# Seven block products per pair: running sums in three PSUM banks, in place of seven buffers

## The chip, the core and the metric

One core of a Trainium2 chip runs the program. The metric is the device time of one execution in microseconds; the kernel before takes 883.73 us (median of three runs, 881.79 to 884.05). TensorE is written PE, VectorE DVE, ScalarE ACT, GpSimd POOL and SyncE SP.

## What is computed

One inference step of a one-layer hybrid recurrent decoder, on 544 tokens (512 of a prompt and 8 x 4 of samples) of width 1024, in float32:

```python
z = x @ p["w_in"]                       # 1024 -> 6144, split among branches and gates gl
out_a = (h * gelu(ya)) @ proj_a         # RG-LRU branch, after a convolution and a scan
out_b = (sb * cu) @ proj_b              # short convolution branch
out_c = (zc * sigmoid(zc @ glu_w + glu_b)) @ proj_c   # S5 state space branch
g = sigmoid(gl)                         # three gates of width 1024
m = g[0] * out_a + g[1] * out_b + g[2] * out_c
x = layer_norm(ALPHA * x + m @ w_out)
f = square(relu(x @ mlp_up)) @ mlp_down # 1024 -> 4096 -> 1024
x = layer_norm(ALPHA * x + f)
```

## The kernel before

Activations lie with channels on the partitions and the 544 tokens along the free axis. To keep float32 accuracy each operand is split into a high half (an ACT cast to fp32r) and a low half (a DVE subtract, value minus high half), and each product is three matmuls: high by high, high by low, low by high. Weights come as tiles of 128 x 1024 (512 KB): SP loads one into one of three raw buffers, ACT casts the high half (`split`, line 809; line 115 for the tiles of other stages), DVE subtracts the low half (line 810; 116), both into one of five weight buffers.

In two stages a group of 256 output channels is computed with a block scheme of seven products in place of eight. These are the gate projections of merge a (three of four quarters) and of merge c (four), and the up projection of the MLP (six of its eight groups of 512 channels, two pairs each): 19 pairs. The weights are cut into quarters A11 to A22, the activations into two halves of the channels and two of the tokens (N1 and N2, 272 tokens each). A pair takes four weight tiles: the first holds A11 and A12 as loaded, the second and third hold sums S1, S2 and S3, S4 that POOL forms from two raw tiles into the buffer "sr" (`p_s` in `add_pair`), the fourth A22. The matching sums of activations (`Tt`) are formed once per stage.

`pair7` is one pair. `prod` gives one product: 4 x 3 matmuls of 128 x 128 by 272 columns (line 844) into a PSUM bank. The order is P1, P2 (first weight tile), P6, P5 (second), P7, P3 (third), P4 (fourth). Each takes a new PSUM buffer by `big()`; there are four such buffers of two banks, which also serve all other matmuls of the stage. ACT copies P1 to p1 in SBUF; DVE adds (line 234, operands "big" and "uu") form u2 = P6 + p1, u4 = P5 + u2, u3 = P7 + u2 and the four result halves in `t` (tile "rl"): t[0] N1 = P2 + p1, t[1] N2 = P7 + u4, t[0] N2 = P3 + u4, t[1] N1 = P4 + u3. After the pair ACT applies tanh (merges) or relu (MLP) to both halves of t.

Weight preparation is a queue, `wq`: `take` gives the next tile, `done` releases one and has `pump` emit the next entry of `prep`, so that five tiles are prepared ahead. So in program order, behind the last product that reads a tile, stands the split of the tile five places on: in the MLP, where each pair is preceded by two tiles of the down projection (96 matmuls, line 147), the release of the pair's second tile (after P5) emits the split of the next pair's first tile. The framework lays out each engine's order from this program by priority and by readiness in its own model, and sets all waits; so an instruction can run ahead of one that is written before it, but only in an order that is fixed when the kernel is built. A wait is on a tile's or bank's earlier readers and writers.

In the merges a pair is followed or preceded by the projection `prj`, whose two PSUM buffers are held until DVE has multiplied them with the gate. In the last quarter of merge a the projection comes first.

Of the kernel before, what the change touches and what calls it, by code (L numbers as in the profile page):

```python
# [11 lines left out]
F32 = mybir.dt.float32  # L12
F32R = mybir.dt.float32r
I32 = mybir.dt.int32
AF = mybir.ActivationFunctionType
ALU = mybir.AluOpType
MUL, ADD, SUB = ALU.mult, ALU.add, ALU.subtract
# [6 lines left out]
H2 = T // 2  # L24
# [10 lines left out]
W2 = 1  # L35
# [30 lines left out]
def kernel(ctx: ExitStack, tc: tile.TileContext, I, O):  # L66
    nc = tc.nc
    V, S, G, PE = nc.vector, nc.scalar, nc.gpsimd, nc.tensor
# [19 lines left out]
    def big():  # L88
        return psb.tile([128, 2, 512], F32, tag="big", name="big")

    def flat(ps):
        return ps[:, :, 0:H2]

    def two(ap):
        return ap.rearrange("p (h n) -> p h n", h=2)
# [85 lines left out]
    for q in range(4):  # L181
# [10 lines left out]
        for e in range(2):  # L192
            k = 2 * q + e
# [39 lines left out]
    def tt(e, o, a, b, op):  # L233
        e.tensor_tensor(o, a, b, op=op)  # L234
# [541 lines left out]
        r.append(t_put(v))  # L776
        return r

    wq = {"prep": [], "n": 0, "live": 0, "t": [], "cap": 4 + W2, "pool": {}, "free": []}

    def pump():
        while wq["live"] < wq["cap"] and wq["n"] < len(wq["prep"]):
            wq["t"].append(wq["prep"][wq["n"]]())
            wq["n"] += 1
            wq["live"] += 1
        if wq["n"] == len(wq["prep"]):
            while wq["live"] < wq["cap"] and wst["sub"] < wst["lim"]:
                w_split(wst["sub"], wq["free"].pop(0))
                wst["sub"] += 1
                wq["live"] += 1  # L790
# [10 lines left out]
    def raw(i, j):  # L801
        w_raw(j)
        return wst["r"][i]

    def split(src, n=1024):
        pool = wq["free"].pop(0)
        h, l = wtile(pool)
        wq["pool"][id(h)] = pool
        S.copy(h[:, 0:n], src)  # L809
        V.tensor_tensor(l[:, 0:n], src, h[:, 0:n].bitcast(F32), op=SUB)  # L810
        return h, l
# [9 lines left out]
    def add_pair(i):  # L821
        sd = {}

        def p_s():
            a, b = raw(i, i), raw(i + 1, i)
            sr = srp.tile([128, 2048], F32, tag="sr", name="sr")
            A11, A12, A21, A22 = a[:, 0:512], a[:, 512:], b[:, 0:512], b[:, 512:]
            S1, S2, S3, S4 = (sr[:, 512 * q:512 * q + 512] for q in range(4))
            tt(G, S1, A21, A22, ADD)
            tt(G, S2, S1, A11, SUB)  # L830
            tt(G, S3, A11, A21, SUB)
            tt(G, S4, A12, S2, SUB)
            sd["s"] = sr
            return split(sr[:, 0:1024])

        wq["prep"] += [lambda: split(raw(i, i)), p_s, lambda: split(sd["s"][:, 1024:]),
                       lambda: split(raw(i + 1, i)[:, 512:], 512)]

    def prod(out, W, o, x):
        h, l = W  # L840
        for k in range(4):
            sl = slice(o + 128 * k, o + 128 * k + 128)
            for oi, (w, y) in enumerate(((h, x[0]), (h, x[1]), (l, x[0]))):
                PE.matmul(out, w[:, sl], y[:, k], start=k == 0 and oi == 0, stop=k == 3 and oi == 2)  # L844

    def pair7(X, Tt):
        t = [ttile(T, "rl") for _ in range(2)]
        uu = upp.tile([128, 4, H2], F32, tag="uu", name="uu")
        p1, u2, u3, u4 = (uu[:, i] for i in range(4))

        def Tx(i):
            return [Tt[i][:, 0], Tt[i][:, 1]]

        def mk():
            return big()[:, 0, 0:H2]

        P1, P2 = mk(), mk()
        Wa = take()
        prod(P1, Wa, 0, [x[:, :, N1] for x in X[0]])
        S.copy(p1, P1)  # L860
        prod(P2, Wa, 512, [x[:, :, N1] for x in X[1]])
        done(Wa)
        tt(V, t[0][:, N1], P2, p1, ADD)
        Ws = take()
        P6 = mk()
        prod(P6, Ws, 512, Tx(1))
        tt(V, u2, P6, p1, ADD)
        P5 = mk()
        prod(P5, Ws, 0, Tx(0))
        done(Ws)  # L870
        tt(V, u4, P5, u2, ADD)
        Wt = take()
        P7 = mk()
        prod(P7, Wt, 0, Tx(2))
        tt(V, u3, P7, u2, ADD)
        tt(V, t[1][:, N2], P7, u4, ADD)
        P3 = mk()
        prod(P3, Wt, 512, [x[:, :, N2] for x in X[1]])
        done(Wt)
        tt(V, t[0][:, N2], P3, u4, ADD)  # L880
        P4 = mk()
        Wz = take()
        prod(P4, Wz, 0, Tx(3))
        done(Wz)
        tt(V, t[1][:, N1], P4, u3, ADD)
        return t

    m = [stile(name="m") for _ in range(2)]
# [25 lines left out]
    def merge7(kh, kl, k4f, pl, out=None):  # L914
        nonlocal ti

        def prj():
            W = take()
            r = []
            for e in range(2):  # L920
                r.append(big())
                k4(outs_flat(r[e]), W, e, kh, kl)
            done(W)
            return r

        for q in range(4):
            if q in k4f:
                ps = prj()
                t = pair7(X0, Tt0)
            elif q in pl:  # L930
                ps, t, g = [], [ttile(T, "t") for _ in range(2)], []
                for e in range(2):
                    g.append(big())
                    W = take()
                    for k in range(KT):
                        sl = slice(k * 128, k * 128 + 128)
                        mm3(outs_flat(g[e]), k == 0, k == KT - 1, W[0][:, sl], W[1][:, sl], *X(k))
                    done(W)
                    S.copy(two(t[e]), flat(g[e]))
                ps = prj()  # L940
            else:
                t = pair7(X0, Tt0)
                ps = prj()
            for e in range(2):
                mt = 2 * q + e
                th, mm = t[e], M_(mt)
                S.activation(th, th, AF.Tanh, scale=0.5)
                V.scalar_tensor_tensor(two(th), two(th), 1.0, flat(ps[e]), op0=ADD, op1=MUL)
                if out is None:
                    tt(G, mm, mm, th, ADD)  # L950
                else:
                    tt(V, th, mm, th, ADD)
                    hd, ld = (x[mt // 4][:, mt % 4] for x in out)
                    S.mul(hd, th, 0.5)
                    V.scalar_tensor_tensor(ld, th, 0.5, hd.bitcast(F32), op0=MUL, op1=SUB)
                run_side(ti)
                ti += 1
# [52 lines left out]
    W = None  # L1010
# [173 lines left out]
    def up_pair(g, q):  # L1184
        if g not in fs:
            fs[g] = ([stile(F32R, name="fh")], [stile(F32R, name="fl")])
        fh, fl = fs[g][0][0], fs[g][1][0]
        t = pair7(X1, Tt1)
        for e in range(2):
            f, v = 2 * q + e, t[e]  # L1190
            S.activation(v, v, AF.Relu)
            S.activation(v, v, AF.Square)
            S.copy(fh[:, f], v)
            tt(V, fl[:, f], v, fh[:, f].bitcast(F32), SUB)
# [252 lines left out]
```

## Time and profile before

| | |
|---|---|
| median of three runs | 883.73 us (881.79, 883.73, 884.05) |
| profiled execution: its time, its span | 883.13 us, 881.4 us |
| PE busy | 841.1 us (95%), 6516 matmuls |
| DVE busy | 635.6 us (72%) |
| ACT busy | 370.7 us (42%) |
| POOL busy | 310.7 us (35%) |
| mean granted TensorE clock | 0.986 of full speed |
| chain that ended last | PE 73%, DVE 15%, POOL 4% of the span |

The span goes from the first to the last instruction. Matmuls are pipelined, and a busy PE need not run at its peak. The chain follows the work back from the last instruction, at each step to what released it. All times in rows are us from the start of the span.

### The profile page before, as it was taken

Reading aid. Unit: us, or ns where it says so; the run is one execution under the profiler, and the core shown is the slowest. Engines: PE = TensorE matmul, PEld = TensorE weight load, DVE = VectorE, ACT = ScalarE, POOL = GpSimd, SP = SyncE. Lnnn points to the kernel's source line nnn. Section 1 sums busy time; section 2 is a strip of 40 time slices with the busy share of each in tenths; the row PEclk is TensorE's granted clock in tenths of the full one; section 3 lists DMA queues with packets and bytes.
Section 4 is the critical chain, followed back from the end, with each engine's and each line's share of the span. In section 5 each row is a group of like instructions: output and inputs, shape, how many; then the busy total and the mean of one; then the engine's idle time right before and its main releaser. Section 6 shows DMA issues by size and latency. Waiting matters only on the chain.

```text
span 881.4 us, 16024 instructions
## 1 busy us (share of the span) xinstructions
PE 841.1 (95%) x6516; PEld 830.7 (94%) x6516; DVE 635.6 (72%) x1032; ACT 370.7 (42%) x626; POOL 310.7 (35%) x293
## 2 busy tenths in 40 slices
PE   7998598989999999979999999999999999999996
PEld 7997497979999999979998999999999999999996
DVE  6976998986756766689857889666666655656656
ACT  4342254253343443444435776344344444444310
POOL 1044853675752454844000321322232213122022
PEclk9999799999999999999999999999999999999998
DMA  8341123121225343223555445333333323223302
GB/s 300 125 113 49 48 79 97 54 75 63 79 72 186 81 138 97 72 72 96 190 176 172 146 137 168 96 97 96 96 97 96 97 95 97 89 88 136 98 2 101
DMA packets 31594, 94.00 MB, mean 107 GB/s; under 512 B 3424, under 2 KB 9952, under 8 KB 31136
## 3 DMA queue, kind: packets, MB, share of 16 engines
q1 hardware_dynamic: 31232, 91.92, 32.9%
q8 instruction: 51, 0.84, 0.4%
q0 software_dynamic: 288, 1.05, 0.3%
q14 instruction: 23, 0.19, 0.1%
HBM read 88.24 MB, written 2.49 MB: 103 GB/s over the span
## 4 chain that ended last, share of the span: by engine, by line
PE 73%; DVE 15%; POOL 4%; issue 3%; ACT 3%; DMA 1%; DVEq 0%; SPq 0%; ACTq 0%; POOLq 0%
PE big L147 45%; PE big L844 22%; DVE wl L116 3%; PE big L1274 1%; PE big L1115 1%; DVE bx L234 1%; DMA raw<-in_w_dram 1%; ACT wh L115 1%; POOL HP L234 1%; DVE cacc L585 1%; POOL sr L234 1%; DVE rl L234 1%; PE big L1056 1%; DVE X L496 1%; POOL Et L234 1%
## 5 line engine op out<-in xcount | busy, mean ns | idle before, releaser
L234 POOL TENSOR_TENSOR sr<-raw 128x512 f32<-128x512 f32 x38 | 61.6, 1641 | 247.5 <-DMA raw<-in_w_dram 206.8
L147 PE MATMUL big<-xh,wh 128*128 128x272 f32 (+2 forms) x544 | 115.4, 294 | 5.5 <-DVE wh L197 4.6
L844 PE MATMUL big<-Tt,wh 128*128 128x272 f32 x608 | 117.1, 289 | 3.6 <-DVE uu L234 1.8
L116 DVE TENSOR_TENSOR wl<-raw,wh 128x1024 fp32r<-128x1024 f32 x70 | 90.2, 1290 | 36.9 <-ACT wh L115 36.9
L147 PE MATMUL big<-xl,wh 128*128 128x272 f32 (+2 forms) x544 | 113.3, 290 | 0.0
L147 PE MATMUL big<-xh,wl 128*128 128x272 f32 (+2 forms) x544 | 113.0, 289 | 0.0
L810 DVE TENSOR_TENSOR wl<-raw,wh 128x1024 fp32r<-128x1024 f32 (+1 forms) x73 | 93.1, 1276 | 16.7 <-ACT wh L809 15.7
L809 ACT CAST wh<-raw 128x1024 fp32r<-128x1024 f32 (+1 forms) x73 | 68.4, 937 | 86.7 <-PE big L147 47.3
L844 PEld LDWEIGHTS big<-Tt,wh 128*128 128x128 f32 x608 | 96.0, 189 | 4.3 <-DVE uu L234 2.0
L115 ACT CAST wh<-raw 128x1024 fp32r<-128x1024 f32 x70 | 73.1, 1047 | 64.0 <-PE big L147 43.6
L147 PE MATMUL big<-fh,wh 128*128 128x272 f32 (+2 forms) x448 | 98.2, 289 | 0.5 <-ACT rl L1168 0.5
L147 PE MATMUL big<-fh,wl 128*128 128x272 f32 (+2 forms) x448 | 97.9, 288 | 0.0
L147 PE MATMUL big<-fl,wh 128*128 128x272 f32 (+2 forms) x448 | 97.7, 288 | 0.0
L147 PEld LDWEIGHTS big<-xh,wh 128*128 128x128 f32 x544 | 85.8, 191 | 6.1 <-ACT xh L196 4.5
L844 PE MATMUL big<-Tt,wl 128*128 128x272 f32 x304 | 88.4, 291 | 0.0
L147 PEld LDWEIGHTS big<-xl,wh 128*128 128x128 f32 x544 | 85.5, 190 | 0.1
L147 PEld LDWEIGHTS big<-xh,wl 128*128 128x128 f32 x544 | 85.3, 190 | 0.0
L810 DVE TENSOR_TENSOR wl<-sr,wh 128x1024 fp32r<-128x1024 f32 x38 | 48.2, 1268 | 36.9 <-ACT wh L809 36.9
L147 PEld LDWEIGHTS big<-fh,wh 128*128 128x128 f32 x448 | 72.4, 188 | 0.7 <-ACT rl L1168 0.7
L147 PEld LDWEIGHTS big<-fl,wh 128*128 128x128 f32 x448 | 72.4, 188 | 0.0
L147 PEld LDWEIGHTS big<-fh,wl 128*128 128x128 f32 x448 | 72.0, 189 | 0.0
L809 ACT CAST wh<-sr 128x1024 fp32r<-128x1024 f32 x38 | 39.6, 1044 | 68.1 <-POOL sr L234 55.0
(299 smaller groups left out, 2088.2 us busy)
## 6 DMA issues: line engine op xcount, KB each, us to landing
raw<-in_w_dram SPq DMA_DIRECT2D x147, 512.0 KB, 3.6
xq<-in_xT_dram SPq DMA_DIRECT2D x2, 1088.0 KB, 6.7
xraw<-in_xT_dram SPq DMA_DIRECT2D x3, 544.0 KB, 7.7
raw<-in_w_dram SPq DMA_DIRECT2D x3, 384.0 KB, 6.6
x<-in_xT_dram SPq DMA_DIRECT2D x2, 576.0 KB, 5.5
U<-us_t SPq DMA_DIRECT2D x16, 68.0 KB, 3.8
zc<-Y SPq DMA_DIRECT2D x16, 68.0 KB, 2.1
bc<-in_bc_dram SPq DMA_DIRECT2D x8, 128.0 KB, 3.3
```

Source lines behind the costliest of these rows:

```text
L115: S.copy(h, r)
L116: V.tensor_tensor(l, r, h.bitcast(F32), op=SUB)
L147: PE.matmul(out, w, x[:, a:b], start=first and oi == 0, stop=last and oi == 2)
L234: e.tensor_tensor(o, a, b, op=op)
L496: V.tensor_tensor_scan(X_[:, r, j], rb, X_[:, r, j], 0.0, op0=MUL, op1=ADD)
L585: V.scalar_tensor_tensor(acc, xp[:, k:568 + k], w(k), acc, op0=MUL, op1=ADD)
L809: S.copy(h[:, 0:n], src)
L810: V.tensor_tensor(l[:, 0:n], src, h[:, 0:n].bitcast(F32), op=SUB)
L844: PE.matmul(out, w[:, sl], y[:, k], start=k == 0 and oi == 0, stop=k == 3 and oi == 2)
L1056: PE.transpose(tp[0:n, ft // 4, o:o + 128], x1[ft // 4][:, ft % 4, c0:c1], ident)
L1115: PE.matmul(out, x, w[:, sl], start=first and kk == 0 and oi == 0, stop=kk == K - 1 and oi == 2)
L1274: PE.matmul(out[:, 256 * e:256 * e + 256], x, w[:, sl], start=False, stop=e == 1 and k == 3 and oi == 2)
```

## The change

`pair7` takes two PSUM buffers for the whole pair and uses three banks of them, PA and PB of the one and PC of the other. PA keeps a running sum: P1, then P6, P7 and P4 accumulate onto it. PB takes P2; PC takes P5, and P3 accumulates onto it. ACT copies PA after P1 (p1) and after P6 (u2), and PC after P5 (p5). Three DVE adds remain: t[0] N1 = PB + p1 (now ahead of the release of the first weight tile), t[1] N2 = PA + p5 after P7, t[0] N2 = PC + u2 after P3. PA after P4 is t[1] N1 itself, and ACT applies the function to it straight from PSUM; the function on t[0] and on t[1] N2 follows in `pair7` too, and the callers drop theirs. In merge a's plain quarter ACT applies tanh straight from PSUM in place of a copy and a tanh afterwards. In the weight queue the four POOL sums of a pair, with the loads of raw weights that they ask for, are emitted right behind the entry ahead of the pair's first split, which is two releases earlier in the program.

```diff
@@ -776,13 +776,17 @@
-    wq = {"prep": [], "n": 0, "live": 0, "t": [], "cap": 4 + W2, "pool": {}, "free": []}
+    wq = {"prep": [], "early": {}, "n": 0, "live": 0, "t": [], "cap": 4 + W2, "pool": {}, "free": []}
 
     def pump():
         while wq["live"] < wq["cap"] and wq["n"] < len(wq["prep"]):
+            if wq["n"] in wq["early"]:
+                wq["early"].pop(wq["n"])()
             wq["t"].append(wq["prep"][wq["n"]]())
             wq["n"] += 1
             wq["live"] += 1
+            if wq["n"] in wq["early"]:
+                wq["early"].pop(wq["n"])()
...
@@ -831,58 +835,52 @@
             tt(G, S3, A11, A21, SUB)
             tt(G, S4, A12, S2, SUB)
             sd["s"] = sr
-            return split(sr[:, 0:1024])
-
-        wq["prep"] += [lambda: split(raw(i, i)), p_s, lambda: split(sd["s"][:, 1024:]),
+
+        wq["early"][len(wq["prep"])] = p_s
+        wq["prep"] += [lambda: split(raw(i, i)), lambda: split(sd["s"][:, 0:1024]), lambda: split(sd["s"][:, 1024:]),
                        lambda: split(raw(i + 1, i)[:, 512:], 512)]
 
-    def prod(out, W, o, x):
+    def prod(out, W, o, x, first=True):
         h, l = W
         for k in range(4):
             sl = slice(o + 128 * k, o + 128 * k + 128)
             for oi, (w, y) in enumerate(((h, x[0]), (h, x[1]), (l, x[0]))):
-                PE.matmul(out, w[:, sl], y[:, k], start=k == 0 and oi == 0, stop=k == 3 and oi == 2)
-
-    def pair7(X, Tt):
+                PE.matmul(out, w[:, sl], y[:, k], start=first and k == 0 and oi == 0, stop=k == 3 and oi == 2,
+                          skip_group_check=not first)
+
+    def pair7(X, Tt, func, scale=1.0):
         t = [ttile(T, "rl") for _ in range(2)]
-        uu = upp.tile([128, 4, H2], F32, tag="uu", name="uu")
-        p1, u2, u3, u4 = (uu[:, i] for i in range(4))
+        p1, u2, p5 = (upp.tile([128, H2], F32, tag=n, name=n) for n in ("p1", "u2", "p5"))
 
         def Tx(i):
             return [Tt[i][:, 0], Tt[i][:, 1]]
 
-        def mk():
-            return big()[:, 0, 0:H2]
-
-        P1, P2 = mk(), mk()
+        ab, cd = big(), big()
+        PA, PB, PC = ab[:, 0, 0:H2], ab[:, 1, 0:H2], cd[:, 0, 0:H2]
         Wa = take()
-        prod(P1, Wa, 0, [x[:, :, N1] for x in X[0]])
-        S.copy(p1, P1)
-        prod(P2, Wa, 512, [x[:, :, N1] for x in X[1]])
+        prod(PA, Wa, 0, [x[:, :, N1] for x in X[0]])
+        S.copy(p1, PA)
+        prod(PB, Wa, 512, [x[:, :, N1] for x in X[1]])
+        tt(V, t[0][:, N1], PB, p1, ADD)
         done(Wa)
-        tt(V, t[0][:, N1], P2, p1, ADD)
         Ws = take()
-        P6 = mk()
-        prod(P6, Ws, 512, Tx(1))
-        tt(V, u2, P6, p1, ADD)
-        P5 = mk()
-        prod(P5, Ws, 0, Tx(0))
+        prod(PA, Ws, 512, Tx(1), False)
+        S.copy(u2, PA)
+        prod(PC, Ws, 0, Tx(0))
+        S.copy(p5, PC)
         done(Ws)
-        tt(V, u4, P5, u2, ADD)
         Wt = take()
-        P7 = mk()
-        prod(P7, Wt, 0, Tx(2))
-        tt(V, u3, P7, u2, ADD)
-        tt(V, t[1][:, N2], P7, u4, ADD)
-        P3 = mk()
-        prod(P3, Wt, 512, [x[:, :, N2] for x in X[1]])
+        prod(PA, Wt, 0, Tx(2), False)
+        tt(V, t[1][:, N2], PA, p5, ADD)
+        prod(PC, Wt, 512, [x[:, :, N2] for x in X[1]], False)
+        tt(V, t[0][:, N2], PC, u2, ADD)
         done(Wt)
-        tt(V, t[0][:, N2], P3, u4, ADD)
-        P4 = mk()
         Wz = take()
-        prod(P4, Wz, 0, Tx(3))
+        prod(PA, Wz, 0, Tx(3), False)
         done(Wz)
-        tt(V, t[1][:, N1], P4, u3, ADD)
+        S.activation(t[0], t[0], func, scale=scale)
+        S.activation(t[1][:, N1], PA, func, scale=scale)
+        S.activation(t[1][:, N2], t[1][:, N2], func, scale=scale)
         return t
 
     m = [stile(name="m") for _ in range(2)]
@@ -926,7 +924,7 @@
         for q in range(4):
             if q in k4f:
                 ps = prj()
-                t = pair7(X0, Tt0)
+                t = pair7(X0, Tt0, AF.Tanh, 0.5)
             elif q in pl:
                 ps, t, g = [], [ttile(T, "t") for _ in range(2)], []
                 for e in range(2):
@@ -936,15 +934,14 @@
                         sl = slice(k * 128, k * 128 + 128)
                         mm3(outs_flat(g[e]), k == 0, k == KT - 1, W[0][:, sl], W[1][:, sl], *X(k))
                     done(W)
-                    S.copy(two(t[e]), flat(g[e]))
+                    S.activation(two(t[e]), flat(g[e]), AF.Tanh, scale=0.5)
                 ps = prj()
             else:
-                t = pair7(X0, Tt0)
+                t = pair7(X0, Tt0, AF.Tanh, 0.5)
                 ps = prj()
             for e in range(2):
                 mt = 2 * q + e
                 th, mm = t[e], M_(mt)
-                S.activation(th, th, AF.Tanh, scale=0.5)
                 V.scalar_tensor_tensor(two(th), two(th), 1.0, flat(ps[e]), op0=ADD, op1=MUL)
                 if out is None:
                     tt(G, mm, mm, th, ADD)
@@ -1185,10 +1182,9 @@
         if g not in fs:
             fs[g] = ([stile(F32R, name="fh")], [stile(F32R, name="fl")])
         fh, fl = fs[g][0][0], fs[g][1][0]
-        t = pair7(X1, Tt1)
+        t = pair7(X1, Tt1, AF.Relu)
         for e in range(2):
             f, v = 2 * q + e, t[e]
-            S.activation(v, v, AF.Relu)
             S.activation(v, v, AF.Square)
             S.copy(fh[:, f], v)
             tt(V, fl[:, f], v, fh[:, f].bitcast(F32), SUB)
```

## Rows read from the trace of the kernel before

**Rows 1.** Windows: start:end, length, then busy us of PE, PEld, DVE, ACT, POOL; clock.

```profile
557.00:848.00 291.00, 291.00 (x2308) 290.99 (x2307) 176.42 (x243) 116.77 (x160) 69.46 (x45) 1.00 0.30 95
340.00:392.00 52.00, 46.96 (x356) 46.07 (x355) 36.32 (x43) 21.24 (x26) 26.84 (x16) 0.97 0.26 81
347.17:358.12 10.95, 10.85 (x86) 10.62 (x86) 8.38 (x13) 3.47 (x5) 4.84 (x4) 1.00 0.29 97
370.15:387.19 17.04, 12.10 (x85) 11.44 (x85) 13.41 (x15) 8.94 (x10) 8.17 (x5) 0.95 0.29 90
```

**Rows 2.** Chain of waits, first pair of the MLP: start, us, what.

```profile
559.92 10.61 PE big L844 x84
```

**Rows 3.** Timeline (start, us, engine, line, operation), last pair of merge a, P3 to P4.

```profile
355.95 0.29 PE L844 MATMUL big<-xh,wl 128*128 128x272 f32 x1
...
356.34 0.30 PEld L844 LDWEIGHTS big<-Tt,wh 128*128 128x128 f32 x2 [0.33 <-DVE rl L234]
...
355.87 0.85 DVE L234 TENSOR_TENSOR rl<-big,uu 128x272 f32<-128x272 f32 x2
```

**Rows 4.** Instructions of line 860: count, duration ns min/median/max.

```profile
L860 ACT COPY uu<-big x19: 368/386/412, 309.5 to 810.5; 128x272 f32<-128x272 f32 x19
```

**Rows 5.** Timeline of ACT in the MLP pair that starts at 605.18.

```profile
606.74 0.39 ACT L860 COPY uu<-big 128x272 f32<-128x272 f32 x1 [0.71 <-PE big L844]
...
611.14 1.06 ACT L809 CAST wh<-raw 128x1024 fp32r<-128x1024 f32 x1 [1.98 <-PE big L844]
```

**Rows 6.** Timelines of DVE and POOL, MLP pairs from 627.79 and from 582.57.

```profile
630.93 0.44 DVE L234 TENSOR_TENSOR rl<-big,uu 128x272 f32<-128x272 f32 x1
631.82 1.23 DVE L810 TENSOR_TENSOR wl<-raw,wh 128x1024 fp32r<-128x1024 f32 x1 [0.44 <-ACT wh L809]
...
634.84 1.23 DVE L810 TENSOR_TENSOR wl<-raw,wh 128x1024 fp32r<-128x1024 f32 x1 [0.52 <-ACT wh L809]
635.98 0.43 DVE L234 TENSOR_TENSOR uu<-big,uu 128x272 f32<-128x272 f32 x1
...
589.61 2.29 DVE L810 TENSOR_TENSOR wl<-raw,wh 128x1024 fp32r<-128x1024 f32 x1 [0.51 <-ACT wh L809]
...
589.54 3.52 POOL L234 TENSOR_TENSOR sr<-raw 128x512 f32<-128x512 f32 x2 [16.24 <-DMA raw<-in_w_dram]
```

**Rows 7.** Windows of line 810 around this subtract, sum over eleven MLP pairs.

```profile
sum 29.70, DVE 17.76; mean DVE 1.61
```

**Rows 8.** Timelines of ACT and DVE, first and second pair of merge a.

```profile
315.97 1.05 ACT L809 CAST wh<-sr 128x1024 fp32r<-128x1024 f32 x1 [0.74 <-POOL sr L234]
...
318.31 0.43 DVE L234 TENSOR_TENSOR uu<-big,uu 128x272 f32<-128x272 f32 x1
...
331.65 2.21 DVE L810 TENSOR_TENSOR wl<-raw,wh 128x1024 fp32r<-128x1024 f32 x1 [0.56 <-ACT wh L809]
```

**Rows 9.** Timeline of DVE, second pair of merge c (from 394.00): u3.

```profile
403.96 0.43 DVE L234 TENSOR_TENSOR uu<-big,uu 128x272 f32<-128x272 f32 x1
```

**Rows 10.** Timelines of PE, ACT and DVE, first pair of merge c (from 370.15).

```profile
376.45 0.52 PE L844 MATMUL big<-Tt,wh 128*128 128x272 f32 x2 [1.76 <-ACT th L1021]
...
384.68 0.52 PE L844 MATMUL big<-Tt,wh 128*128 128x272 f32 x2 [1.77 <-DVE uu L234]
...
376.26 0.41 ACT L860 COPY uu<-big 128x272 f32<-128x272 f32 x1
380.76 1.16 ACT L1025 ACTIVATE ch<-th 128x544 fp32r<-128x544 f32 x1 [4.09 <-DVE th L1022]
...
381.96 1.19 DVE L1026 SCALAR_TENSOR_TENSOR cl<-th,ch 128x544 fp32r<-128x544 f32 x1 [0.88 <-ACT ch L1025]
```

**Rows 11.** Waits, all engines: who waited for whom, us in total, times, longest.

```profile
POOL sr L234 <- DMA raw<-in_w_dram: 206.8, 16, 22.1
```

**Rows 12.** Windows after the first and the third wait of rows 10.

```profile
376.45:379.45 3.00, 3.00 (x24) 3.00 (x24) 3.00 (x3) 0.22 (x1) 2.92 (x2) 1.00 0.00 0
384.70:390.00 5.30, 5.30 (x30) 5.30 (x31) 4.79 (x8) 1.57 (x4) 0.00 (x0) 0.68 0.31 102
```

## The prediction

> **What bounds the kernel now.** I read the table of engines first, then the windows by stage, then the chain, then the timeline of single pairs. TensorE (PE) is busy for 841.1 us of the span of 881.4, DVE for 72% of it and ACT for 42%. The 19 block pairs lie between 307 and 438 us (7 of them, in the merges) and between 557 and 848 us (12, in the MLP). In the MLP PE is busy for all of 291.00 us; in the merges the stretch 340 to 392 alone has idle time, 5.04 us [rows 1]. The chain of waits says the same: from 559.92 on it is PE after PE, a pair of 84 matmuls in 10.61 us (10.58 in most) [rows 2]. A matmul thus takes 0.126 us and a product of twelve 1.51. So there are some 5 us to win, at one place, and each new wait of PE elsewhere is paid in full. All 19 pairs are judged by one question: does a PSUM bank come free before PE wants it again?
>
> **The deadline.** One pair of before has only two buffers to work in, the last of merge a, since its projections hold the other two [rows 3]. P3's last matmul started at 355.95, so P4's first was due at 356.08. Its weight load waited for a DVE add that ended at about 356.30 (355.87 plus half of the 0.85 of two), and started at 356.34. The pair took 10.95 us [rows 1], 0.37 over 10.58. A release that is 0.22 late thus costs 0.37: it is in time only 0.15 before the product is due. From here on I count from the pair's start in the chain (347.17 here). P4 is due at 8.91, its deadline is 8.76; with 1.51 a product it is 7.25 for P3, 5.74 for P7 and 2.72 for P6.
>
> **What the change removes.** Four DVE adds of 0.43 us a pair [rows 6], 33 us of DVE in all, and two ACT copies where merge a takes its plain quarter. Neither engine is the bound, so this is worth nothing by itself. PSUM demand falls from seven buffers in rotation to two: worth something only where PE waited for one, in the first pair of merge c (below).
>
> **What it adds.** Two ACT copies of 0.39 us a pair [rows 4] and one more ACT instruction, since the function is applied in three pieces: some 1.2 us of ACT, beside an ACT that stands idle for 2 us between a pair's casts [rows 5]. And it adds four waits of PE within each pair:
> - P6 waits for the copy of P1. That copy starts at 1.56 and is done at 1.95 [rows 5]; deadline 2.72: nothing.
> - P7 waits for the copy u2 of P1 + P6, ready at about 4.6. ACT is idle then [rows 5], so it is done at 5.0; deadline 5.74: nothing.
> - P3 waits for the copy p5. At the same place stands the cast that refills the second weight tile. It writes the high half alone, whose last reader is P5's last matmul but one, so it starts at 5.96 [rows 5], while P5's result is there at about 6.1. I take it that the cast goes first, since the order on the engines follows readiness: the first add of the pair runs ahead of a subtract that is written before it [rows 6]. The cast ends at 7.01, the copy at about 7.31 (two such run with an overlap of 0.09): 0.06 late.
> - P4 waits for the DVE add of P7 to p5. On DVE the subtract of that same refill stands before it, as it stands before u3 now [rows 6]. So the new add gets the place of u3: it starts 0.09 before the subtract's end and takes 0.43.
>
> The last wait decides. In the MLP the subtract starts at 7.05 (7.30 in the first pair) and takes 1.23 us, but 2.29 where POOL was already forming the next sums [rows 6]. The add ends at 7.05 + its time + 0.34, so the loss is its time less 1.37. Over eleven pairs these subtracts sum to 17.76 us [rows 7]: five are of 1.22 or 1.23, and six of 1.38 to 2.29 hold the other 11.6, so they lose 11.6 − 6 × 1.37 = 3.4. The first pair starts late: 0.1 more. The twelfth has a plain refill: none. With 0.06 from p5 in the pairs that lose nothing: 4.0 us in the MLP.
>
> In merge a's first pair the refill is a POOL sum, which reaches ACT at 315.97; u3's place ends at 318.74, or 10.79 from the pair's start at 307.95: 2.0 us [rows 8]. In its second the subtract takes 2.21 from 331.65 on: 0.9 [rows 8]. The third loses its 0.37 no more (one add less before the deadline), but the bank of P4 is now freed by ACT, behind two casts, where the next stage wants it: 0.3 net, a guess. In merge c's second pair DVE is behind with the output's splits and u3 ends at 404.39 [rows 9]; less 0.88 for the two adds that are gone, 9.51 from the start at 394.00: 0.75. The third is like it: 0.75. The fourth: none. Together 4.7.
>
> Merge c's first pair takes 17.04 us [rows 1], since PE waits three times for a buffer, among it 1.76 for ACT and 1.77 for u2 on DVE [rows 10]. With two buffers needed these go; but P6 must now wait for the copy of P1, which ACT ends at 376.67, while it would be wanted at 372.9. And what follows the pair needs the gate's last split, which leaves DVE at 383.15 [rows 10]. Bounds: 6.3 gained if all waits go, 1 lost if ACT does u2 and p5 behind the gate's work. I take 1.5 gained, nearer to the loss, for ACT's order stays.
>
> **Early POOL sums.** Four POOL adds a pair and SP's load of one raw weight move two refills up. POOL waited 206.8 us for raw weights to land [rows 11], not for its turn, and the load waits for one of three raw buffers; neither gets sooner. I count 0. If the sums did start sooner, they would leave the critical subtract alone (3.4 gained), or meet it in the short pairs too (5 × 0.9 = 4.5 lost).
>
> **Sum.** 4.0 + 4.7 − 1.5 = 7.2 us on the profiled execution's 883.13 (its span is 881.4), which lies 0.60 below the median of the three runs: 890.3.
>
> **Rivals.** (1) *The copy p5 goes before the cast.* The subtract is then ready 0.4 later, at about 7.45, and finds POOL's second operation running where it now finds the first or none: losses of 0.3 without POOL and 0.7 to 1.3 with it, 10.7 in the MLP and 6 in the merges, less 1.5: 898. For it: the copy is written first; against: the cast is ready first. (2) *The add overtakes the subtract.* It is ready at 7.6, the subtract at 7.05 or 7.45, so this wants the copy first and an order that errs by 0.2. Nothing is lost then but in the merges: 883 to 885, no difference. (3) *Faster.* As in rival 2, and merge c's first pair falls to about the length of the others. Where ACT does u2 and p5 decides it: within the 4.09 us in which it now waits for the gate's DVE step [rows 10], or behind that. 883.1 − 6.3 + 2 = 879. (4) *The two banks of a buffer count as one for the waits.* P2 then waits for the copy of P1 and P6 for the first add, each some 0.45 + 0.15: 1.2 × 19 = 23, so 906. No row of before shows one bank of a buffer written while the other is read.
>
> (5) *The clock falls.* After the wait of 1.76 us the granted clock was 1.00; after the last of the three waits it was 0.68 over 5.30 us, partly at the lower level of 1.2 GHz, and 30 matmuls ran where 42 fit: 1.5 us [rows 12]. If the eight waits of 0.7 us and more did that each time: 12 more, 902. The Trainium skill, page "TensorE: Matmul & The Clock Gate", section "HAM oscillation — how this bites in real kernels", speaks for this rival: waits that return at every step can throttle the array at every step. The trace speaks against it: the wait of 1.76 us left the clock alone, and so did the one that cost 0.37.
>
> **How the numbers follow.** Forecast 0.46 (886 to 894); rival 1 0.18; rival 2 0.18; rival 3 0.11; rivals 4 and 5 0.07 together. The range, 880.5 to 901, holds the forecast and rivals 1 and 2, and leaves most of 3, 4 and 5 out. A measurement of this kernel tells about 0.3% (2.65 us) from no change. Faster than 881.1: rival 3 and an edge of 2, 0.13. Within: most of rival 2 and the forecast's lower edge, 0.22. Slower: 0.65.
>
> **What would show it.** Right: pairs of 10.6 to 11.6 us in the chain in place of 10.58, PE's weight load waiting for a DVE add into "rl" with a weight subtract right before that add, the copy p5 behind a cast on ACT, and about 4 us of idle PE in the MLP where there is none. Wrong: the copy p5 ahead of the cast (rival 1), the add ahead of the subtract and no idle PE (rival 2), P2 waiting for ACT (rival 4), or a lower clock in the MLP (rival 5).

## The result: 906.4 us, and the profile after

The changed kernel takes 906.38 us (median of four runs, 904.95 to 906.74) where the kernel before takes 882.76 (four runs, 880.66 to 884.05): 1.0276 times as long, 95% interval 1.0256 to 1.0296. The forecast was 7.2 us more, and the range ended at 901; the loss is 23.6 us. The profiled execution took 906.74 us, with a span of 905.0. The price of rival 4 (906) fits and its mechanism turned out to be the main one, though not at the sizes that were written beside it.

In the code printed after the change the product's matmul is line 848, the copies of p1, u2 and p5 are 862, 868 and 870 (tiles "p", "u", "p"), a refill's cast and subtract are 813 and 814, and the three adds are on line 234 ("rl" from "big" and "p" or "u").

Windows by stage, the merges with what follows them (from the first product to the first MLP pair), and the MLP (to its last product), first of before, then of after; columns as in [rows 1]:

```profile
307.80:559.80 252.00, 246.50 (x1855) 240.36 (x1853) 193.43 (x272) 129.82 (x190) 78.77 (x49) 0.99 0.42 131
559.80:819.00 259.20, 259.20 (x2065) 259.20 (x2065) 160.56 (x223) 108.88 (x149) 69.46 (x45) 1.00 0.32 101
```

```profile
308.20:573.00 264.80, 253.34 (x1854) 243.15 (x1853) 184.91 (x244) 134.08 (x211) 78.95 (x49) 0.98 0.39 124
573.00:843.20 270.20, 270.12 (x2070) 261.78 (x2069) 148.28 (x176) 117.68 (x186) 69.33 (x45) 1.00 0.31 98
```

The merges grew by 12.8 us and the MLP by 11.0. The granted clock is 0.98 and 1.00, where it was 0.99 and 1.00, and DVE has some 21 us less to do. PE counts as busy for all but 0.1 us of the MLP, but its weight loads (second pair of numbers) no longer do. So the view to read is that of the weight loads' waits, in the MLP (first three lines) and in the merges (the other three); columns: us in total, times, longest.

```profile
PEld big L848 <- DVE rl L234: 3.5, 17, 0.3
PEld big L848 <- ACT p L862: 1.4, 7, 0.2
PEld big L848 <- ACT u L868: 1.2, 6, 0.2
...
PEld big L848 <- DVE rl L234: 8.3, 9, 2.8
PEld big L848 <- ACT p L862: 5.1, 7, 3.7
PEld big L848 <- ACT u L868: 2.0, 5, 1.1
```

The kernel before had none of these in the MLP. In the merges it had three kinds, 2.0 us each, where now there are 15.4. The MLP has thirty waits of about 0.2 us, and the view leaves the shortest out: by the starts of PE's matmuls all twelve pairs stall before P2, P6, P7 and P4, 48 times and 10.6 us in all (2.6, 2.9, 2.6 and 2.5 by product). The timeline of the weight loads in the MLP's third pair shows one full set of four:

```profile
622.06 0.19 PEld L848 LDWEIGHTS big<-x1h,wh 128*128 128x128 f32 x1 [0.20 <-ACT p L862]
624.43 0.30 PEld L848 LDWEIGHTS big<-Tt,wh 128*128 128x128 f32 x2 [0.20 <-DVE rl L234]
626.68 0.30 PEld L848 LDWEIGHTS big<-Tt,wh 128*128 128x128 f32 x2 [0.20 <-ACT u L868]
629.95 0.30 PEld L848 LDWEIGHTS big<-Tt,wh 128*128 128x128 f32 x2 [0.21 <-DVE rl L234]
```

The first is P2, which reads "x1h": it goes to PB, an untouched bank, and yet it waits for the copy of P1 out of PA. The second is P6, which accumulates onto PA, whose copy is long done; it waits for the first add, which reads PB. The third is P7, waiting for the copy u2 of the bank that it accumulates onto. The fourth is P4, waiting for the add of P7. What one such wait costs is seen where PE and DVE stand side by side at the second:

```profile
624.17 0.28 PE L848 MATMUL big<-Tt,wl 128*128 128x272 f32 x1
624.44 0.52 PE L848 MATMUL big<-Tt,wh 128*128 128x272 f32 x2
624.79 0.28 PE L848 MATMUL big<-Tt,wl 128*128 128x272 f32 x1
...
623.94 0.44 DVE L234 TENSOR_TENSOR rl<-big,p 128x272 f32<-128x272 f32 x1 [1.75 <-PE big L848]
```

The add ends at 624.38; PE's next matmul was due at 624.30 and starts at 624.44, and the two that follow take 0.35 us in place of 0.25. A release 0.08 late thus costs 0.24, which is the deadline rule of the prediction (0.08 + 0.15). The four stalls of a pair cost mostly 0.17 to 0.25 each, P4's 0.14 to 0.35. The chain of waits, which had the first MLP pair in one piece of 10.61 [rows 2], now has for it:

```profile
573.16 6.58 PE big L848 x48
579.74 0.12 PE big L147
579.86 4.92 PE big L848 x36
```

That is 11.62 us for 85 matmuls, 0.9 more than 85 of 0.126. Twelve pairs at 0.8 to 1.1 make up nearly all of the MLP's 11.0.

The order of PE has changed too: the framework, which lays the waits into its model, seems to fill them with other matmuls. In the timeline of the first pair the first matmuls of P5 ("Tt") stand ahead of P2 ("x1h"), and a lone matmul of the down projection (line 147) ahead of P7:

```profile
574.95 0.29 PE L848 MATMUL big<-Tt,wh 128*128 128x272 f32 x1
575.21 0.39 PE L848 MATMUL big<-x1h,wh 128*128 128x272 f32 x1
...
579.58 0.28 PE L147 MATMUL big<-fh,wh 128*128 128x272 f32 x1
579.85 0.52 PE L848 MATMUL big<-Tt,wh 128*128 128x272 f32 x2
```

Nine of P5's twelve matmuls stand ahead of P6, so P7 comes four matmuls behind P6 (the last three of P5 and the lone one) and not twelve, and has to wait for u2. Every second pair has another order: all of P5 stands ahead of P6, eleven of P3's matmuls ahead of P7, and P4 comes five matmuls behind P7. Rows of ACT, PE and DVE in the second pair:

```profile
603.08 1.05 ACT L813 CAST wh<-raw 128x1024 fp32r<-128x1024 f32 x1 [1.05 <-PE big L848]
604.03 0.38 ACT L868 COPY u<-big 128x272 f32<-128x272 f32 x1
...
604.47 0.52 PE L848 MATMUL big<-Tt,wh 128*128 128x272 f32 x2
...
606.28 0.44 DVE L234 TENSOR_TENSOR rl<-big,p 128x272 f32<-128x272 f32 x1 [0.31 <-PE big L848]
```

There P7 (604.47) waits because the copy u2 stands behind a cast, and P4 waits for an add that itself waited for P7: the subtract before it had ended 0.31 us earlier.

In the merges the same waits are long, because ACT and DVE have other work there; two of them, the first and the third pair of merge c:

```profile
380.11 0.29 PEld L848 LDWEIGHTS big<-xh,wh 128*128 128x128 f32 x1 [3.72 <-ACT p L862]
...
425.65 0.30 PEld L848 LDWEIGHTS big<-Tt,wh 128*128 128x128 f32 x2 [2.83 <-DVE rl L234]
...
423.47 1.78 DVE L952 SCALAR_TENSOR_TENSOR ml<-rl,mh 128x544 fp32r<-128x544 f32 x1
425.17 0.43 DVE L234 TENSOR_TENSOR rl<-big,p 128x272 f32<-128x272 f32 x1
```

At 380.11 P2 waits for a copy that stands behind the gate's work on ACT. At 425.65 P6 waits 2.83 us for the first add, which stands behind the output's split on DVE: a result that nobody needs for long, from a bank that P6 doesn't write.

### The profile page after: what moved, and what is told of

The parts are those of the page before. It is cut to its first block, busy times and chain, and to the rows that moved or that the text cites. A ratio compares the mean times of both kernels' runs of the same rounds, so it can differ in the third digit from the quotient of the medians.

```text
span 905.0 us, 15992 instructions
## 1 busy us (share of the span) xinstructions
PE 858.7 (95%) x6516; PEld 835.9 (92%) x6516; DVE 613.6 (68%) x956; ACT 381.9 (42%) x681; POOL 312.3 (35%) x293
## 4 chain that ended last, share of the span: by engine, by line
PE 69%; DVE 16%; issue 5%; POOL 5%; ACT 3%; DMA 2%; SPq 1%; DVEq 0%; POOLq 0%; ACTq 0%
PE big L147 42%; PE big L848 20%; DVE wl L116 3%; PE big L1112 2%; POOL sr L234 2%; DVE wl L814 2%; DMA raw<-in_w_dram 2%; PE big L1270 1%; DVE bx L234 1%; DVE rl L234 1%; POOL HP L234 1%; DVE Tt L752 1%; DVE cacc L585 1%; SPq L528 1%; PE big L1053 1%
## 5 line engine op out<-in xcount | busy, mean ns | idle before, releaser
L234 POOL TENSOR_TENSOR sr<-raw 128x512 f32<-128x512 f32 x38 | 57.9, 1547 | 260.4 <-DMA raw<-in_w_dram 244.0
L848 PE MATMUL big<-Tt,wh 128*128 128x272 f32 x608 | 128.0, 300 | 7.4 <-DVE rl L234 6.2
L814 DVE TENSOR_TENSOR wl<-raw,wh 128x1024 fp32r<-128x1024 f32 (+1 forms) x73 | 95.7, 1311 | 28.6 <-ACT wh L813 27.4
L1197 DVE SCALAR_TENSOR_TENSOR x<-x,big 128x544 f32<-128x544 f32 x48 | 34.3, 719 | 51.8 <-PE big L147 51.1
```

Of the source, the lines that this page charges most:

```text
L848: PE.matmul(out, w[:, sl], y[:, k], start=first and k == 0 and oi == 0, stop=k == 3 and oi == 2, skip_group_check=not first)
L1197: V.scalar_tensor_tensor(dst, dst, ALPHA if g == 0 else 1.0, flat(ps), op0=MUL, op1=ADD)
```

## The experiments

Each is compared with runs of the kernel before on the same chip; where a number is a median, the ratio to before and its 95% interval stand beside it. Not all experiments ran on the same chip: where the difference of two is given, a figure in brackets behind it first takes each from the kernel before on its own chip. In the edited kernels a line can have a number that is a few lower or higher.

### A buffer for each bank

```diff
-        ab, cd = big(), big()
-        PA, PB, PC = ab[:, 0, 0:H2], ab[:, 1, 0:H2], cd[:, 0, 0:H2]
+        PA, PB, PC = (big()[:, 0, 0:H2] for _ in range(3))
```

> The changed kernel with one edit: P2 gets a buffer of its own, so the pair uses three buffers and no two of its sums share one. Theory S (waits are kept per buffer, so P2 waits for ACT's copy of P1, and P6 waits for DVE's add that reads P2): both waits go in all 19 pairs. In the MLP that is 2 of about 4 waits of some 0.24 us, 0.5 us x 12 = 6 us; in merge c the waits of 1.8 to 2.8 us for the add go, some 7 us: about 893 us, and PE no longer works on other products between P1 and P2. Theory R (the cost is the reuse of banks as such, copies and adds before P7, P3 and P4): P2 and P6 cost little, no more than 2 us less, 904.

Measured: 896.71 us, 1.0183 [1.0158, 1.0208], 9.7 (8.5) less than the changed kernel, and nearer to theory S than to theory R. The merges take 256.7 us (4.7 more than before), the MLP 267.5 (8.3 more). Of the waits in the MLP the one for the add remains, nine times (columns as above):

```profile
PEld big L848 <- DVE rl L234: 7.2, 9, 0.9
```

That one is the wait of P4 which the forecast rested on. The second MLP pair, timelines of ACT, DVE, POOL and the weight load:

```profile
592.34 1.05 ACT L813 CAST wh<-raw 128x1024 fp32r<-128x1024 f32 x1 [1.00 <-PE big L848]
593.29 0.38 ACT L869 COPY p<-big 128x272 f32<-128x272 f32 x1
...
593.42 2.22 DVE L814 TENSOR_TENSOR wl<-raw,wh 128x1024 fp32r<-128x1024 f32 x1 [1.80 <-ACT wh L813]
595.57 0.43 DVE L234 TENSOR_TENSOR rl<-big,p 128x272 f32<-128x272 f32 x1
...
593.26 3.52 POOL L234 TENSOR_TENSOR sr<-raw 128x512 f32<-128x512 f32 x2 [16.27 <-DMA raw<-in_w_dram]
...
596.04 0.30 PEld L848 LDWEIGHTS big<-Tt,wh 128*128 128x128 f32 x2 [0.78 <-DVE rl L234]
```

The copy p5 stands behind the cast, the add behind the subtract, the subtract is lengthened by POOL, and P4 waits: every step as forecast, and neither rival 1 nor rival 2. The same subtract is over 2.1 us in nine of the eleven pairs (2.12 to 2.36), where the trace of before had four over 2 (2.09 to 2.29). By the forecast's own rule (time less 1.37) nine that sum to 20.1 us lose 7.8.

### Two products in one buffer, in the kernel before

```diff
-        P1, P2 = mk(), mk()
+        ab = big()
+        P1, P2 = ab[:, 0, 0:H2], ab[:, 1, 0:H2]
```

> The kernel before with one edit: P1 and P2 take the two banks of one buffer; all else, the seven DVE adds and the order, as before. Theory S: P2 waits for ACT's copy of P1 in each of 19 pairs, 0.2 to 0.4 us each, 4 to 8 us: 887 to 891 us. Theory R (the bank is the unit of the waits): P2 waits for nothing, 882 to 884.

Measured: 885.32 us, 1.0049 [1.0029, 1.0069], 3.7 more than before. The waits, first in the MLP, then in the merges:

```profile
PEld big L844 <- ACT uu L861: 1.2, 6, 0.2
...
PEld big L844 <- ACT uu L861: 6.8, 7, 5.4
```

P2 waits for the copy of P1 as soon as the two share a buffer, in a kernel that has nothing else of the change. So this wait belongs to the buffer, not to the running sums. By the medians the price is just under the 4 to 8 us of theory S; by the windows it is 4.7 (2.4 in the merges, 2.3 in the MLP). PE is given four to seven other matmuls to do between P1 and P2 here too.

### The early POOL sums alone, and the change without them

```diff
+            if wq["n"] in wq["early"]:
+                wq["early"].pop(wq["n"])()
...
-        wq["prep"] += [lambda: split(raw(i, i)), p_s, lambda: split(sd["s"][:, 1024:]),
+        wq["early"][len(wq["prep"])] = p_s
+        wq["prep"] += [lambda: split(raw(i, i)), lambda: split(sd["s"][:, 0:1024]), lambda: split(sd["s"][:, 1024:]),
```

> The kernel before with the early POOL sums alone; pair7 is as before. My forecast counted this part at 0: 882 to 884 us, POOL's sums start when they did. Rival: the early emission moves loads or POOL work to worse places in merge a, where the first pair came out 2.9 us longer: 885 to 886.

> The changed kernel without the early POOL sums; pair7 is the new one. If that part is worth nothing: 905 to 907 us. If it hides part of the new pair's cost: 908 or more; if it is part of the cost: 903 or less.

The first, the kernel before with this part alone: 881.90 us, 1.0006 [0.9992, 1.0019]. The second, the change without it: 907.07 us, 1.0298 [1.0276, 1.0319]. The part is worth nothing either way, and none of the loss is its.

### The release written behind the add

```diff
-        done(Ws)
         Wt = take()
         prod(PA, Wt, 0, Tx(2), False)
         tt(V, t[1][:, N2], PA, p5, ADD)
+        done(Ws)
```

> x1_own_buffer with one more edit: the release of the second weight tile (and so the cast and the subtract of its refill) is written behind the DVE add of P7, so the subtract no longer stands ahead of the add for which P4 waits. In x1 the MLP has 7.2 us of such waits in 9 pairs, and its pairs took 8.3 us longer than before. Theory A (that subtract, at 2.1 to 2.3 us beside POOL's sums, is what P4 waits for): the MLP takes 259 to 260 us again and the whole 886 to 889. Rival: the refill that comes later starves a later product, or the add waits for something else: 894 or more.

> The changed kernel with that edit alone (P1 and P2 still share a buffer). Its waits of PE on the add before P4 are about 0.2 us in half of the pairs, so theory A expects little here: 902 to 905. If the order laid down by the builder were the cause of all, it would come down to 895.

With a buffer for each bank: 893.12 us, 1.0116 [1.0091, 1.0141]. On the changed kernel: 906.13 us, 1.0260 [1.0226, 1.0294]. Both miss, and not because the theory of the add is wrong: in the first there are still eight such waits (6.6 us), the subtract still before the add. Where an instruction is written doesn't set its place on DVE here: DVE has the same order with and without the edit, from the first pair to the last. So the runs show that this edit doesn't do what it says. With a buffer for each bank the kernel is all the same 3.6 us (4.3) faster with it, and the two intervals don't meet; the profiled executions differ by 1.1. What makes that difference is open, and it is a warning: differences of 3 to 4 us between two experiments on different chips show little here.

### The other bank shared

```diff
-        PA, PB, PC = ab[:, 0, 0:H2], ab[:, 1, 0:H2], cd[:, 0, 0:H2]
+        PA, PB, PC = ab[:, 0, 0:H2], cd[:, 1, 0:H2], cd[:, 0, 0:H2]
```

> The changed kernel with P2 in the second bank of PC's buffer in place of PA's: as many buffers and banks as the change. Theory S (a buffer is the unit of the waits): P2 does not wait for the copy of P1, P6 does not wait for the add that reads P2; only P5, a product later, waits for that add. As x1_own_buffer: 895 to 899. If x1 won by its third buffer and not by the pairing: 904 to 907.

> Both edits of x5 with two buffers (x7 and the release behind the add). Theories S and A together: as x5, 886 to 889.

Measured: 898.76 us, 1.0183 [1.0151, 1.0214], within what theory S wanted; with the release written later 899.01, 1.0176 [1.0147, 1.0206], which misses for the same reason as above. PB now shares with PC, so P5 and not P6 has to wait for the first add, 1.5 us later. In the MLP that is enough: 265.0 us, with six waits of P4 (4.8 us) beside six long subtracts, and no short ones. In the merges it isn't: in the profiled execution, 901.75 us and the longest of the four, they take 264.8 us as with the change, and the waits for the add there come to this:

```profile
PEld big L848 <- DVE rl L234: 7.9, 5, 2.6
```

So two buffers don't hold three sums for free in either pairing.

### The subtract pinned behind the add

```diff
-        tt(V, t[1][:, N2], PA, p5, ADD)
+        add = V.tensor_tensor(t[1][:, N2], PA, p5, op=ADD)
+        with tc.issue_after(getattr(add, 'ins', add)):
+            done(Ws)
```

Here `done(Ws)` is taken from its old place, and what it emits is ordered behind the add.

> x1_own_buffer, with the subtract of the second tile's refill pinned behind the DVE add of P7 in DVE's order (moving its release in the program left the order as it was). Theory A (P4 waits for that add only since the subtract stands before it): the 6.6 to 7.2 us of waits in the MLP go, its pairs take 259.5 to 261 us from the first to the last matmul where x1 took 267.5, and the whole 887 to 890. Rival (the add is late for another reason, P7's end or the copy p5): no more than 2 us less, 893 or more.

> The changed kernel with that pin alone; P1 and P2 share a buffer. Of the four waits in an MLP pair only the one before P4 goes: 0.15 to 0.25 us in half of the pairs or more, 2 to 3 us: 903 to 905. If the shared buffer did not matter by itself, it would come to the time of x9.

With a buffer for each bank: 886.66 us, 1.0057 [1.0037, 1.0076], 10.1 (10.8) less than without the pin and just under the 887 to 890. The MLP takes 260.0 us, 0.8 more than before, and the view of waits lists none in it. ACT, DVE and PE in the second MLP pair:

```profile
591.45 0.38 ACT L869 COPY p<-big 128x272 f32<-128x272 f32 x1
...
592.21 0.44 DVE L872 TENSOR_TENSOR rl<-big,p 128x272 f32<-128x272 f32 x1 [2.43 <-PE big L848]
592.57 1.27 DVE L814 TENSOR_TENSOR wl<-raw,wh 128x1024 fp32r<-128x1024 f32 x1
...
591.82 0.29 PE L848 MATMUL big<-Tt,wl 128*128 128x272 f32 x1
591.94 0.34 PE L848 MATMUL big<-x1h,wh 128*128 128x272 f32 x1
592.12 0.29 PE L848 MATMUL big<-x1l,wh 128*128 128x272 f32 x1
```

The add is first now and the subtract, 0.4 us later, does no harm. P3's first matmul takes 0.34 in place of 0.29, and the next starts 0.05 late: that fits the copy p5, which ended at 591.83, and the 0.06 that the forecast put on it.

On the changed kernel the same pin gives 905.97 us, 1.0269 [1.0250, 1.0288]: 0.4 (0.0) less, and not the 2 to 3 that were expected. The stall before P4 was small there to begin with (2.5 us in the MLP, against 7.6 with three buffers), since the three stalls ahead of it put P4 off more than the subtract. And the pin takes it away in the six pairs of the first order alone (11.4 us each for some 11.65). In the second order P4 still waits for the add, which waits for P7's end; DVE and the weight load in the second pair:

```profile
604.76 0.44 DVE L873 TENSOR_TENSOR rl<-big,p 128x272 f32<-128x272 f32 x1 [3.35 <-PE big L848]
...
605.25 0.30 PEld L848 LDWEIGHTS big<-Tt,wh 128*128 128x128 f32 x2 [0.20 <-DVE rl L873]
```

So the two causes don't add: the pin is worth 10.1 us (10.8) with three buffers and 0.4 (0.0) with two, and the shared buffer costs 19.3 with the pin and 9.7 (8.5) without.

### The new pair in the MLP alone

Own buffers and pin as before in the MLP; in the merges the pair of the kernel before (`pair7o`), with the function applied in it (at both of its calls there):

```diff
-                t = pair7(X0, Tt0, AF.Tanh, 0.5)
+                t = pair7o(X0, Tt0, AF.Tanh, 0.5)
```

> x9 in the MLP and the pair of before (seven buffers, seven adds) in the merges. The MLP as in x9, the merges as before (252 us from the first pair to the MLP): 882 to 885. It tells what the new pair costs in the merges by itself: x9 less this run.

Measured: 883.09 us, 1.0006 [0.9994, 1.0018]. What the new pair costs in the MLP can't be told from nothing (0.75 us in the whole, and the interval includes no change), and in the merges it costs 3.6 us (886.66 less 883.09, on one chip). Nor does it win anything: four DVE adds fewer in each of twelve pairs, and no time. No kernel of this study was faster than the one before.

### A buffer for each bank, without the early sums

```diff
-        ab, cd = big(), big()
-        PA, PB, PC = ab[:, 0, 0:H2], ab[:, 1, 0:H2], cd[:, 0, 0:H2]
+        PA, PB, PC = (big()[:, 0, 0:H2] for _ in range(3))
...
-        wq["early"][len(wq["prep"])] = p_s
+        wq["prep"] += [lambda: split(raw(i, i)), p_s, lambda: split(sd["s"][:, 1024:]),
```

> The change with PB in a buffer of its own, and without the early POOL sums (the weight queue is that of before). It asks why nine of eleven subtracts of the second tile's refill were long with a buffer for each bank (896.7 us), where the forecast took the lengths of the kernel before (4.0 us lost). Theory E, the early sums let POOL start tenths of a us sooner, just ahead of the subtract, in the pairs where it started just behind it: without them four to six of the eleven are long again, PE waits for the add of P7 four to six times, some 4 us in the MLP, and the time is 892 to 893. Theory L, POOL starts when the raw weight has landed whatever the order of issue, and a pair that is stretched by a wait gives the transfer more time before the next: eight to ten are long, 7 us of waiting, 896 to 897.5.

Measured: 895.08 us, 1.0149 [1.0126, 1.0172]; the waits in the MLP:

```profile
PEld big L844 <- DVE rl L234: 6.8, 9, 0.9
```

Nine again, with 6.8 us, as theory L wants. The time, 1.6 (2.0) less than with the early sums, lies between the two theories, and the two intervals overlap; a part of 1 to 3 us for the early sums isn't excluded, but the number of long subtracts doesn't come from them. Nor is theory L's second half shown, that a stretched pair makes the next subtract long: in the kernel before with the early sums alone no pair is stretched, and nine of eleven take over 2 us as well.

## Why the prediction was wrong, step by step

**What bounds the kernel, and the deadline: right.** PE is the bound, each wait in the MLP is paid in full, and a release costs its lateness plus 0.15 (0.24 for 0.08 here). Removed DVE adds are worth nothing: shown by the new pair in the MLP alone.

**The list of four new waits, from "P6 waits for the copy of P1 … nothing" on: this step failed.** It listed the waits by bank, while the kernel's waits are by buffer: PA and PB are two banks of one, so P2 also waits for the copy of P1 and P6 for the first add. The prediction named this as rival 4, worked its price out as 906, and gave it a part of the 0.07 that rivals 4 and 5 have together, with the remark that no row of before shows one bank of a buffer written while the other is read. That absence spoke neither for nor against it. The description of the kernel says that a wait is on "a tile's or bank's" readers, and the forecast took the second word where the two banks are one tile. Moving P2 alone into P1's buffer in the kernel before shows the wait; giving PB its own buffer takes it away. Price: 9.7 us (8.5) by the one comparison, 19.3 by the other. With that buffer the kernel takes 896.71, which the range holds; what is left over the 890.3 is the matter of the points on P4 and on the merges below.

**Rival 4's own sum was right by luck, by offsetting errors.** It had two waits a pair at 0.60, 14.4 us in the MLP. There its two, P2 and P6, measure 5.5, and the stalls of P7 and P4 bring the MLP to 11.0; the merges lost 12.8 where it had 8.4, since there the waits are for adds and copies queued behind other work.

**"P7 waits for the copy u2 … nothing": failed as a consequence.** The step took PE's order as given. In the changed kernel nine to twelve matmuls of P5 stand ahead of P6, so P6 ends 1.1 to 1.5 us later beside its stalls; P7 then comes four matmuls behind P6, and in every second pair the copy u2 stands behind a cast. With three buffers the order stays and P7 doesn't wait in the MLP: no wait for "u" is left there. What the shared buffer would cost in the old order is open: no run of the new pair has the one with the other.

**The wait of P4: right in mechanism, too small by half.** Copy behind cast, add behind subtract: with three buffers seen as written, and gone when the subtract is pinned behind the add. In the changed kernel itself the other stalls hide most of it (2.5 us are left, and in six pairs the subtract is done before the add is due). The term was 4.0 us; with three buffers the MLP lost 8.3 (267.5 less 259.2). (Its parts add up to 3.9, and the 0.1 for the first pair is a slip: counted like the others, from the chain's start, that subtract starts at 7.13 and not 7.30, and the pair lost nothing to P4.) Its rule held (7.8 from nine lengths); what failed was taking the lengths from the one trace of before. Which subtracts are long is decided by who starts first. In the kernel before, the subtract at 589.61 came 0.07 after POOL's sum at 589.54 and took 2.29, and the one at 634.84 took 1.23 [rows 6], since POOL came 0.11 after it and was itself held, 2.27 for a sum that takes 1.28 alone:

```profile
634.95 2.27 POOL L234 TENSOR_TENSOR sr<-raw 128x512 f32<-128x512 f32 x1 [17.55 <-DMA raw<-in_w_dram]
```

POOL starts when its raw weight lands, so two tenths of a microsecond in a transfer make a pair long or short. The trace of before showed four of eleven over 2 us; the profiles after it in which that subtract is not pinned and the buffers are not shared as in the change show six to nine. The upper end, all eleven long, was in the text only as a remark on the early sums (4.5 us more), and that remark's size was right: 4.0 + 4.5. Why POOL starts earlier relative to the pair in one run than in another is not settled; the early sums aren't needed for it, since nine are long without them too.

**The merges: 3.2 forecast, 4.7 measured** with three buffers and no pin, which is the kernel that the forecast reckoned with (3.6 with the pin, against the same with the old pair there). In the order of the pairs the terms were 2.0, 0.9, 0.3, then −1.5, 0.75, 0.75 and 0; from the first to the last matmul of each pair the losses are 0.9, 1.0, 0.2, then 0.8, 0.9, 0.9 and 0.1. So three of the waits for the add came as forecast (0.90, 0.73 and 0.75 in the view), the first pair of merge a waits 0.87 for the copy u2 instead, and the term that was wrong is the 1.5 us to be won in the first pair of merge c: that pair lost 0.8, and 2.4 in the profile with the pin. With three buffers and the pin, the waits in the merges are:

```profile
PEld big L848 <- ACT p L861: 3.6, 1, 3.6
PEld big L848 <- ACT u L867: 3.2, 2, 2.0
PEld big L147 <- ACT rl L882: 0.6, 1, 0.6
```

The first pair of merge c there, ACT and the two weight loads (P6, P7):

```profile
375.48 0.40 ACT L861 COPY p<-big 128x272 f32<-128x272 f32 x1
...
375.93 0.30 PEld L848 LDWEIGHTS big<-Tt,wh 128*128 128x128 f32 x2 [3.65 <-ACT p L861]
...
382.48 0.30 PEld L848 LDWEIGHTS big<-Tt,wh 128*128 128x128 f32 x2 [1.96 <-ACT u L867]
```

P6 waits for the copy of P1, which ACT does behind the gate's work, and P7 for u2. They took the place of the waits of before [rows 10]. The third line is the bank of P4 freed by ACT at the end of merge a, guessed at 0.3 net; here PE waits 0.6 for it.

**The early sums at 0, and the clock: right.** Rival 5 isn't seen: with 48 stalls in the MLP the granted clock there is 1.00.

## What to carry to other kernels

Count a wait by what the builder tracks, not by what the memory could do: two values that live at different times want two buffers, and a packed buffer joins the readers of both. When a new wait is listed, ask what the builder's scheduler will do with the order around it, and don't price the next steps on the old order; where an order matters, pin it, for a line moved in the program moved nothing on DVE here. Where a cost depends on a race that nobody waits for yet, take the worst case of it as the bound, for one trace shows one throw.

## What the runs showed of the hardware

A wait that is short still costs a fixed part: 0.08 us late gave 0.24 us. The matmul started 0.06 after the add's end, 0.14 late, and the next two took 0.35 in place of 0.25; that second part, 0.10, is there at each of the 48 stalls.

The lengthened subtract ends at a fixed time after POOL's start: with a buffer for each bank POOL begins at 593.26 and the subtract ends at 595.64, in the kernel before at 589.54 and 591.90 [rows 6], so 2.38 and 2.36, about one POOL sum (1.28 alone) and one subtract (1.23) less 0.15. In all six pairs of these two traces in which POOL's first sum starts up to 0.3 ahead of the subtract, the time is 2.36 to 2.38. So it seems not to share the time with POOL, but to wait for one whole sum and then to run; POOL's 2.27 at 634.95 is the same the other way round. The Trainium skill, page "SBUF — State Buffer", section "Who interferes with whom", says much the same: a DVE operation with two inputs in SBUF contends with a GpSimd operation that reads SBUF, over a pair of ports that is locked by one at a time, and one with at most one SBUF input, outside the two-port modes, doesn't. The runs agree with both halves: the add from PSUM at 595.57, beside POOL's second sum, took 0.43.

That P2 waits for P1's reader is not the chip's doing so far as these runs go: with a buffer for each bank PE writes PB while ACT copies PA (in the second MLP pair the copy goes from 588.26 to 588.63, and P2's matmuls start from 587.73 on). That shows it for two banks of different buffers; for two banks of one buffer no run shows it. The Trainium skill, page "PSUM — Partial Sum Buffer", section "PSUM bank collisions raise a hardware error", likewise has accesses to different banks run side by side; the unit in which this kernel waits is larger than that.
